# A hybrid trunk on one core: products 6 and 7 set apart by a quarter, the multiplications by embedding weights in ordered steps, the residual's copy behind the copies of the first product

## The chip, the cores and the metric

The kernel runs on one core of one Trainium2 chip. The metric is the time of one execution on the device, in microseconds (us); smaller is better. Before the change three runs took 1029.31, 1035.53 and 1035.87 us, with a median of 1035.53. The engines have short names in the profile: PE multiplies matrices, DVE is the vector engine, ACT the scalar engine, POOL the general one, which here mostly issues DMAs, and SP issues the loads of weights.

## The reference

Two layers over 256 tokens of 2048 features, in float32. An even layer (HGRN2 and RG-LRU side by side) and an odd one (mLSTM) are each followed by an output projection onto the residual and by a gated embedding of each layer's own. Cut to what matters:

```python
D_MODEL = 2048; SEQ = 256; DEPTH = 2; PLE_DIM = 256
h = x
for i in range(DEPTH):
    hn = rmsnorm(h, e_norm[j] if i % 2 == 0 else o_norm[j])
    if i % 2 == 0:
        u = hn @ e_w_in[j]
        ...
        y = jnp.concatenate([ya, yb], axis=-1).astype(h.dtype)
        mix = y @ e_w_out[j]
    else:
        u = hn @ o_w_in[j]
        ...
        yc = (head_rmsnorm(yc, c_norm[j]) * jax.nn.sigmoid(og.astype(jnp.float32))
              * jax.nn.silu(z.astype(jnp.float32)))
        mix = yc.astype(h.dtype) @ o_w_out[j]
    h = h + mix
    pl = rmsnorm(p[i].astype(h.dtype) @ ple_w[i], ple_norm[i])
    h = h + jax.nn.sigmoid(h @ ple_gate_w[i]) * pl
return rmsnorm(h, final_norm)
```

## The kernel before

**How weights become products.** A weight is float32 and is used as a sum of a high and a low half. SP loads a piece of 128 x 1024 into a tile `raw` (a ring of five), ACT casts it to the high half `whi` (L136, or L218 in the products below), and DVE subtracts to get the low half `wlo` (L137, L219). Both halves have rings of four. The activations `ahl` are split in the same way. PE then makes three matmuls of 128 x 512 for each product of two pieces: high by high, low by high, high by low (L208 to L210, or L232). A stop of PE therefore has a chain behind it: a cast on ACT, a subtraction on DVE.

**Plain blocks and seven products.** A projection works on blocks of 512 columns. Its first blocks are plain: four quarters of the 2048 features, one after the other. Pairs of blocks go through `seven` (L283), which replaces the eight products of a 2 x 2 split of one quarter (or of two) by seven, made of sums of weight pieces and of activations (`combos`, L246, whose results are the tiles `q`), and treats the remaining quarters plainly. It has four PSUM banks: A, F and B of the pool called `mm`, and E of the pool called `mx`. Every pair starts with the first product into A. ACT then copies A to F (L335) and -F to B (L336), where `home` is given also the residual tile to E (L338), and the second product goes into E. The rest follows a string, one letter at a time: a digit is that product (5, 6 and 7 into B, 2 into A, 4 into F), a or b is a plain quarter of the first block (into A and F) or the second (into E and B), A or F hands that result on, and a dot is a call of `pump`. Product 5's and product 6's sums in B are copied out by ACT (`keep`, L317), product 7's is subtracted by DVE (`soon`, L313).

**The four uses.** The string for one quarter, `ORDERS[1]`, is used by the even output projection (weights `in_eo`), the gate of the first embedding (`in_g0`), the first pair of the odd layer's output gates (`in_oog`) and the odd output projection (`in_oo`). Only the last gives `home`: there E starts from a quarter of the residual, `hq[3]`, which the odd layer has stored to DRAM and loads back on POOL's queue (`hq<-dh`).

**What sets the order.** Each engine runs its instructions in a fixed order, which a scheduler makes from the dependences and from priorities (`high_priority`). `issue_after(x)` keeps an instruction behind x on x's engine. Work of other kinds sits in generators, one per lane; each `pump` takes one step of every lane and keeps its instructions behind the last ones noted for each engine:

```python
def pump():
    with ExitStack() as behind:
        for ins in last.values():
            behind.enter_context(tc.issue_after(ins))
        for lane in list(lanes):
            step(lane)
```

One such lane is `pg`: the multiplications of the first layer's embedding by its norm's weights (`ple_gain`, L541). Another brings finished parts of the residual from token-major to feature-major form, by a hop through DRAM on POOL's queue (`across`, L669: one store at L672 and four loads into `r` at L675). The weights of the norm come by `row` (L532): two DMAs on POOL's queue, each of which spreads half a row over all partitions. `row` was called where the lane is started, so its DMAs were no step and had no place kept. The sums of the next layer's gates (`gate_sums`, L1134, matmuls at L1140) are a step of a lane too.

Of the kernel before, what the change touches and what calls it, by code (L numbers as in the profile page):

```python
# [15 lines left out]
AF = mybir.ActivationFunctionType  # L16
# [6 lines left out]
KT = D // P  # L23
EPS = 1e-6
RSQRT_MAGIC = 0x5F3759DF
ORDERS = {1: "a5a6.7b2.4aAFbb", 2: "a5.2aA64.7F.bb"}


_PRM = [
# [15 lines left out]
def trunk(ctx: ExitStack, tc: tile.TileContext, a, out):  # L45
    nc = tc.nc
    v, s, gp, te, sy = nc.vector, nc.scalar, nc.gpsimd, nc.tensor, nc.sync
# [17 lines left out]
    def start(lane, gen):  # L65
        lanes.setdefault(lane, []).append(gen)
# [9 lines left out]
# [6 lines that stand above are left out]
# [40 lines left out]
    def block(src, c, n):  # L122
        return src[c * P:(c + n) * P].rearrange("(p n) -> p n", p=P)
# [90 lines left out]
    def split_weights(r):  # L214

        hi, lo = (wp.tile([P, 1024], F32R, name=n, tag=n) for n in ("whi", "wlo"))
        with tc.high_priority(offset=400):
            last["act"] = s.copy(hi, r).ins  # L218
            last["dve"] = v.tensor_tensor(out=lo, in0=r, in1=hi.bitcast(F32), op=ALU.subtract).ins  # L219
        return hi, lo  # L220

    def product(o, stat, parts, first=False, end=False):

        n = 2 * len(parts)
        for k in range(n):
            xh, xl = (x[k] for x in stat)
            wh, wl = (x[:, (k % 2) * 512:(k % 2 + 1) * 512] for x in parts[k // 2])
            for i, (x, y) in enumerate(((xh, wh), (xh, wl), (xl, wh))):
                with ExitStack() as behind:
                    if k + i == 0:  # L230
                        behind.enter_context(tc.issue_after(last["pe"]))
                    last["pe"] = te.matmul(o, x, y, start=(first and k + i == 0), stop=(end and k == n - 1 and i == 2),  # L232
                                           skip_group_check=True).ins

    def stationary(act, js, hf):
        return [[tokens(act[j][x], k, hf) for j in js for k in range(2)] for x in range(2)]

    def plain(w, j, kq, act, ps, first=(False, False), end=False):

        parts = load_weights(w[4 * j + kq])  # L240
        for hf in range(2):
            product(ps[hf], stationary(act, (2 * kq, 2 * kq + 1), hf), parts, first[hf], end)
            if hf == 0:
                pump()
# [38 lines left out]
    def seven(w, j, act, qs, kqs, room, part, home=None, order=None):  # L283

        def src(b, side, kq):
            return block(w[4 * (j + b) + kq], side * 1024, 1024)

        def load(tile_of, b, side):
            tiles = []
            for kq in kqs:  # L290
                t = tile_of()
                sy.dma_start(out=t, in_=src(b, side, kq))
                tiles.append(t)
            return tiles

        def ring():
            return wp.tile([P, 1024], F32, name="raw", tag="raw", bufs=5)

        def split(tiles):
            return [split_weights(t) for t in tiles]  # L300

        def add(x, y):
            with tc.high_priority(offset=400):
                for xi, yi in zip(x, y):
                    v.tensor_tensor(out=xi, in0=xi, in1=yi, op=ALU.add)

        def add_loaded(x):
            for xi, kq in zip(x, kqs):
                gp.dma_start(out=xi, in_=src(1, 0, kq), accum_op=ALU.add)

        def soon(out, in0, in1, op):
            with tc.high_priority(offset=450):
                v.tensor_tensor(out=out, in0=in0, in1=in1, op=op)  # L313

        def keep(out, bank):
            with tc.high_priority(offset=450):
                s.copy(out, bank)  # L317

        def quadrant(side, hf):
            return stationary(act, [2 * kq + side for kq in kqs], hf)  # L320

        def combo(n):
            return [[t for kq in kqs for t in qs[n, kq][x]] for x in range(2)]

        acc = len(kqs) == 2
        rest = [kq for kq in range(4) if kq not in kqs]
        E = px.tile([P, 512], F32, name="mx", tag="mx")
        A, F, B = (pm.tile([P, 512], F32, name="mm", tag="mm") for _ in range(3))
        b5, g = part(), part()
        X = load(room, 0, 0)  # L330
        product(A, quadrant(0, 0), split(X), True)
        if acc:
            add_loaded(X)
        with tc.high_priority(offset=450):
            s.copy(F, A)  # L335
            s.activation(B, F, AF.Copy, scale=-1.0)  # L336
            if home is not None:
                s.copy(E, home)  # L338
        Y = load(room, 1, 1)
        product(E, combo(4), split(Y), home is None)  # L340
        W = X
        if not acc:
            W = load(ring, 1, 0)
            add(Y, W)
            add(W, X)
        rows = [list(rest), list(rest)]
        did = set()
        for op in order or ORDERS[len(kqs)]:
            if op in "ab":
                b = "ab".index(op)  # L350
                kq = rows[b].pop(0)
                plain(w, j + b, kq, act, ((A, F), (E, B))[b], end=not rows[b])
            elif op == "5":
                product(B, combo(1), split(W))
                add(X, Y)
                if acc:
                    add_loaded(Y)
                keep(b5, B)
            elif op == "6":
                product(B, combo(2), split(X))  # L360
                keep(g, B)
            elif op == "2":
                Z = load(ring, 0, 1)
                product(A, quadrant(1, 0), split(Z))
            elif op == "4":
                product(F, quadrant(1, 1), split(X))
            elif op == "7":
                product(B, combo(3), split(Y))
                soon(b5, B, b5, ALU.subtract)
            elif op == ".":  # L370
                pump()
            elif op == "A":
                yield 0, 0, A
            elif op == "F":
                soon(b5, F, b5, ALU.subtract)
                yield 0, 1, b5
            did.add(op)
            if op in "26" and {"2", "6"} <= did:
                add(X, Z)
        if home is None:  # L380
            soon(g, E, g, ALU.add)
            yield 1, 0, g
        else:
            soon(home, E, g, ALU.add)
            yield 1, 0, None
        yield 1, 1, B
# [145 lines left out]
    def row(pool, tag, bufs, i):  # L532

        halves = []
        for b in range(2):
            t = pool.tile([P, 1024], F32, name="row", tag=tag, bufs=bufs)
            gp.dma_start(out=t, in_=a["rows"][i, b * 1024:(b + 1) * 1024].partition_broadcast(P))
            halves.append(t)
        return halves

    def ple_gain(pls, rows):  # L541
        yield
        for g in range(4):
            for pl in pls[g]:
                v.tensor_tensor(out=pl, in0=pl, in1=rows[g // 2][:, (g % 2) * 512:(g % 2 + 1) * 512], op=ALU.mult)
                yield

    def to_features(h, c, act, gain, name, more=None):

# [64 lines left out]
    def small(n, name, rows=P):  # L614
        return cp.tile([rows, n], F32, name=name)
# [7 lines left out]
    pls = embed(a["pw"], None, lambda: p0.tile([P, 512], F32, name="pl", tag="pl"),  # L623
                lambda: sy.dma_start(out=prm, in_=a["prm"]))
# [82 lines left out]
    def gate_tok(w, j, act, u):  # L707
# [7 lines left out]
    mx, e0, e1, lb, omb, sp, ez, z2, pol, sp8, spm8 = (small(8, n) for n in (  # L715
        "mx", "e0", "e1", "lb", "omb", "sp", "ez", "z2", "pol", "sp8", "spm8"))
# [402 lines left out]
    pe0 = []  # L1119
    act = out_proj(hq, mixed(), "fe")  # L1120
    e0 = pe0[0]
    start("pg", ple_gain(pls, row(e0, "row", 2, 0)))

    gr = e0.tile([P, KT, 16], F32, name="gr")
    sy.dma_start(out=gr, in_=a["ogf"])
# [45 lines left out]
    with tc.tile_pool(name="m1", bufs=2) as m1:  # L1171
# [198 lines left out]
        def part():  # L1370
            n = len(turn) % 4
            turn.append(n)
            return store_of[n // 2][:, n % 2 * 512:(n % 2 + 1) * 512]
# [7 lines left out]
        def pair(w, jj, two):  # L1381
            return seven(w, jj, acth, qs, (0, 1) if two else (0,), chain2 if two else chain, part)
# [51 lines left out]
        pls = embed(a["pw1"], pact, pl_half)  # L1434
# [250 lines left out]
```

## Time and profile before

| | us |
|---|---|
| median of three runs | 1035.53 |
| lowest and highest run | 1029.31, 1035.87 |
| the profiled execution | 1035.23 |
| its span, first to last instruction | 1033.5 |
| busy: DVE, ACT, POOL | 824.0, 650.9, 105.2 |

The span is what the page covers; the 1.7 us between it and the execution's time lie around it. In a timeline a row is: start, duration, engine, line and operation, result <- operands, shapes, count, and in brackets how long the engine had been idle and what ended that. Matmuls overlap: one lasts 0.39 us, but a running PE starts the next before that has ended, so intervals are taken from start to start. Where a row of the kernel before names L545, L590 or L703, the kernel after has the same work two lines further down.

### The profile page before, as it was taken

What the parts mean: (1) busy time and instruction counts of PE and PEld (TensorE: products, weight loads), DVE (VectorE), ACT (ScalarE), POOL (GpSimd) and SP (SyncE); (2) the same over time, 40 slices, a digit from 0 to 9 for tenths busy, and PEclk for the clock granted to TensorE, in tenths of its full rate; (3) what the DMA queues carried; (4) which work ended last, traced back from release to release, by engine and by line L of the source; (5) the groups of instructions that cost most, each with busy time, mean ns of one, the idle gap of its engine ahead of it and who ended that gap; (6) DMA issues with size and microseconds to landing.
All of it is one profiled execution on the core that took longest, in us unless ns stands there. A gap on an engine that the chain in (4) does not pass through costs nothing.

```text
span 1033.5 us, 14486 instructions
## 1 busy us (share of the span) xinstructions
PE 1015.4 (98%) x5170; PEld 840.6 (81%) x5170; DVE 824.0 (80%) x1208; ACT 650.9 (63%) x933; POOL 105.2 (10%) x190
## 2 busy tenths in 40 slices
PE   9999999999999899999999999999999998999996
PEld 8888888888888778878888888888888886878886
DVE  7858968969685898888559987878889995986684
ACT  7675555586964455676557876666676866454562
POOL 0111101011111111022021100001001120102000
PEclk9999999999999999999999999999999999999999
DMA  9987756567688698588798756466879796679652
GB/s 363 328 232 243 224 165 204 184 194 243 225 258 310 210 314 267 167 290 277 242 287 243 232 175 202 126 231 186 284 184 289 220 283 259 197 256 283 229 184 82
DMA packets 69672, 242.14 MB, mean 234 GB/s; under 512 B 9024, under 2 KB 10432, under 8 KB 69600
## 3 DMA queue, kind: packets, MB, share of 16 engines
q1 hardware_dynamic: 54720, 193.36, 57.0%
q0 software_dynamic: 14448, 47.33, 16.6%
q8 instruction: 40, 0.66, 0.3%
q10 hardware_dynamic: 432, 0.52, 0.1%
q14 instruction: 32, 0.26, 0.1%
HBM read 221.26 MB, written 19.92 MB: 233 GB/s over the span
## 4 chain that ended last, share of the span: by engine, by line
PE 90%; DMA 4%; ACT 1%; DVE 1%; issue 1%; POOL 1%; ACTq 0%; DVEq 0%; POOLq 0%
PE mm L232 21%; PE mm L208 16%; PE mm L209 16%; PE mm L210 16%; PE mx L232 5%; PE mx L209 3%; PE mx L210 3%; PE mx L208 3%; DMA hq<-dh 2%; DMA ducn<-w 1%; DMA row<-in_rows_dram 1%; PE nu L1319 1%; PE mm L1510 1%; PE mm L1509 1%; PE mm L1511 1%
## 5 line engine op out<-in xcount | busy, mean ns | idle before, releaser
L136 ACT CAST whi<-raw 128x1024 fp32r<-128x1024 f32 (+1 forms) x317 | 331.1, 1048 | 229.3 <-PE mm L210 115.7
L137 DVE TENSOR_TENSOR wlo<-raw,whi 128x1024 fp32r<-128x1024 f32 (+1 forms) x317 | 381.4, 1213 | 115.2 <-ACT whi L136 106.7
L208 PE MATMUL mm<-whi,ahl 128*128 128x512 f32 x768 | 300.3, 391 | 0.0
L209 PE MATMUL mm<-wlo,ahl 128*128 128x512 f32 x768 | 299.3, 390 | 0.0
L210 PE MATMUL mm<-whi,ahl 128*128 128x512 f32 x768 | 298.9, 389 | 0.0
L232 PE MATMUL mm<-whi,ahl 128*128 128x512 f32 x552 | 177.1, 390 | 0.0
L208 PEld LDWEIGHTS mm<-whi,ahl 128*128 128x128 f32 x768 | 144.2, 188 | 30.3 <-issue 0.4
L210 PEld LDWEIGHTS mm<-whi,ahl 128*128 128x128 f32 x768 | 144.2, 188 | 30.2
L209 PEld LDWEIGHTS mm<-wlo,ahl 128*128 128x128 f32 x768 | 144.2, 188 | 29.8 <-DVE wlo L137 0.8
L232 PEld LDWEIGHTS mm<-whi,ahl 128*128 128x128 f32 x552 | 103.6, 188 | 22.1 <-issue 0.4
L232 PE MATMUL mm<-wlo,ahl 128*128 128x512 f32 x276 | 107.6, 390 | 1.4 <-DVE wlo L137 1.4
L219 DVE TENSOR_TENSOR wlo<-ch,whi 128x1024 fp32r<-128x1024 f32 x56 | 67.5, 1218 | 7.6 <-ACT whi L218 6.3
L218 ACT CAST whi<-ch 128x1024 fp32r<-128x1024 f32 x56 | 58.4, 1050 | 17.9 <-PE mm L232 10.7
L208 PE MATMUL mx<-whi,ahl 128*128 128x512 f32 x160 | 62.9, 393 | 2.9 <-ACT whi L136 2.9
L209 PE MATMUL mx<-wlo,ahl 128*128 128x512 f32 x160 | 63.3, 395 | 2.0 <-DVE wlo L137 2.0
L210 PE MATMUL mx<-whi,ahl 128*128 128x512 f32 x160 | 62.8, 393 | 0.0
L232 PEld LDWEIGHTS mm<-wlo,ahl 128*128 128x128 f32 x276 | 51.8, 188 | 12.6 <-DVE wlo L137 1.8
L232 PE MATMUL mx<-whi,ahl 128*128 128x512 f32 x144 | 47.3, 389 | 0.0
L232 PE MATMUL mm<-whi,q 128*128 128x512 f32 x120 | 41.0, 394 | 2.7 <-ACT pr L317 2.7
L208 PEld LDWEIGHTS mx<-whi,ahl 128*128 128x128 f32 x160 | 30.4, 190 | 9.8 <-ACT whi L136 3.4
L209 PEld LDWEIGHTS mx<-wlo,ahl 128*128 128x128 f32 x160 | 30.4, 190 | 9.1 <-DVE wlo L137 2.7
L210 PEld LDWEIGHTS mx<-whi,ahl 128*128 128x128 f32 x160 | 30.5, 190 | 6.3
(377 smaller groups left out, 1229.5 us busy)
## 6 DMA issues: line engine op xcount, KB each, us to landing
raw<-in_ew_dram SPq DMA_DIRECT2D x64, 512.0 KB, 5.1
raw<-in_g_dram SPq DMA_DIRECT2D x62, 512.0 KB, 4.8
raw<-in_oqk_dram SPq DMA_DIRECT2D x32, 512.0 KB, 5.4
raw<-in_ov_dram SPq DMA_DIRECT2D x32, 512.0 KB, 3.7
raw<-in_eo_dram SPq DMA_DIRECT2D x30, 512.0 KB, 5.3
raw<-in_oo_dram SPq DMA_DIRECT2D x30, 512.0 KB, 6.0
raw<-in_oog_dram SPq DMA_DIRECT2D x24, 512.0 KB, 4.3
raw<-in_oz_dram SPq DMA_DIRECT2D x20, 512.0 KB, 4.9
```

What stands on the lines that cost most here:

```text
L136: last["act"] = s.copy(h, r).ins
L137: last["dve"] = v.tensor_tensor(out=l, in0=r, in1=h.bitcast(F32), op=ALU.subtract).ins
L208: te.matmul(ps[hf], xh, wh, start=(k == 0), stop=False)
L209: te.matmul(ps[hf], xh, wl, start=False, stop=False)
L210: last["pe"] = te.matmul(ps[hf], xl, wh, start=False, stop=(k == KT - 1)).ins
L218: last["act"] = s.copy(hi, r).ins
L219: last["dve"] = v.tensor_tensor(out=lo, in0=r, in1=hi.bitcast(F32), op=ALU.subtract).ins
L232: last["pe"] = te.matmul(o, x, y, start=(first and k + i == 0), stop=(end and k == n - 1 and i == 2), skip_group_check=True).ins
L1319: te.matmul(ps[:, 0:n], x[:, i, o:o + P], y[:, b, i], start=(b == 0 and x is sh and y is vh), stop=(b == hf and y is vl))
L1509: te.matmul(o, xh, wh, start=(k == 0), stop=False)
L1510: te.matmul(o, xh, wl, start=False, stop=False)
L1511: last["pe"] = te.matmul(o, xl, wh, start=False, stop=(k == KT - 1)).ins
```

## The change

It has three parts.

The string for one quarter has a new order. Product 2, a quarter of the first block and A's result now stand between products 6 and 7; product 4 comes behind 7 and a quarter of the second block; and there is one dot more.

The residual's copy into E is now issued behind the second of ACT's two copies of the first product.

`ple_gain` gets a function in place of the tiles. The load of the row is now the lane's first step, with a step of its own, and the multiplications go two to a step.

```diff
-ORDERS = {1: "a5a6.7b2.4aAFbb", 2: "a5.2aA64.7F.bb"}
+ORDERS = {1: "a5a6.2aA7b.4F.bb", 2: "a5.2aA64.7F.bb"}
...
             s.copy(F, A)
-            s.activation(B, F, AF.Copy, scale=-1.0)
-            if home is not None:
-                s.copy(E, home)
+            with tc.issue_after(s.activation(B, F, AF.Copy, scale=-1.0).ins):
+                if home is not None:
+                    s.copy(E, home)
...
-    def ple_gain(pls, rows):
+    def ple_gain(pls, load):
+        rows = load()
+        yield
         yield
         for g in range(4):
             for pl in pls[g]:
                 v.tensor_tensor(out=pl, in0=pl, in1=rows[g // 2][:, (g % 2) * 512:(g % 2 + 1) * 512], op=ALU.mult)
-                yield
+            yield
...
-    start("pg", ple_gain(pls, row(e0, "row", 2, 0)))
+    start("pg", ple_gain(pls, lambda: row(e0, "row", 2, 0)))
```

**PE in the even output projection.** Before, the rows go from product 6 to product 7 and on to b; both products are into bank B, which is `mm_3423` here, and E is `mx_3420`. The operands `q4_3148` and `q4_3096` are sums of activations.

```order
L232 MATMUL mm_3423<-wlo_3539,q4_3148 128x512
L232 MATMUL mm_3423<-whi_3538,q4_3148 128x512
L232 MATMUL mm_3423<-whi_3549,q4_3096 128x512
L232 MATMUL mm_3423<-wlo_3550,q4_3096 128x512
L232 MATMUL mm_3423<-whi_3549,q4_3096 128x512 x2
L232 MATMUL mm_3423<-wlo_3550,q4_3096 128x512
L232 MATMUL mm_3423<-whi_3549,q4_3096 128x512
L232 MATMUL mx_3420<-whi_3561,ahl_2981 128x512
```

After the change the same place reads as follows; `mm_3421` is bank A.

```order
L232 MATMUL mm_3423<-wlo_3539,q4_3148 128x512
L232 MATMUL mm_3423<-whi_3538,q4_3148 128x512
L232 MATMUL mm_3421<-whi_3551,ahl_2791 128x512
L232 MATMUL mm_3421<-wlo_3552,ahl_2791 128x512
L232 MATMUL mm_3421<-whi_3551,ahl_2791 128x512 x2
L232 MATMUL mm_3421<-wlo_3552,ahl_2791 128x512
L232 MATMUL mm_3421<-whi_3551,ahl_2791 128x512
L232 MATMUL mm_3421<-whi_3563,ahl_3297 128x512
```

Product 2 follows product 6, then the 24 matmuls of a quarter a into A and F (the last row is its first), and only then product 7 into B. The other three uses have the same order.

**DVE, from the even output projection to the first gate.** Before, the first two multiplications by the row stood between two pairs of `wlo` of the even output projection:

```order
L1034 TENSOR_TENSOR xr<-r,tt 128x512 x2
L151 TENSOR_TENSOR ahl<-xr,ahl 128x2x256 x2
L137 TENSOR_TENSOR wlo<-raw,whi 128x1024 x2
L545 TENSOR_TENSOR pl<-pl,row 128x512 x2
L137 TENSOR_TENSOR wlo<-raw,whi 128x1024 x2
L590 TENSOR_TENSOR hq<-mm,hq 128x512
```

After, all eight stand in the first gate:

```order
L137 TENSOR_TENSOR wlo<-raw,whi 128x1024
L572 TENSOR_TENSOR ahl<-r,ahl 128x256 x4
L137 TENSOR_TENSOR wlo<-raw,whi 128x1024 x4
L547 TENSOR_TENSOR pl<-pl,row 128x512 x5
L137 TENSOR_TENSOR wlo<-raw,whi 128x1024
L547 TENSOR_TENSOR pl<-pl,row 128x512
L137 TENSOR_TENSOR wlo<-raw,whi 128x1024
L572 TENSOR_TENSOR ahl<-r,ahl 128x256 x4
L547 TENSOR_TENSOR pl<-pl,row 128x512 x2
```

The other six were in the first gate before as well, one or two at a time between pairs of `wlo`. The first four of the eight read the first half of the row, the other four the second. On POOL the two row DMAs stood ahead of the first hop of the even output projection, and stand behind its fourth and last hop now.

**ACT in the odd output projection.** Before, the residual's copy stood among casts of plain quarters:

```order
L436 ACTIVATE sq,pss<-pl 128x512 x3
L136 CAST whi<-raw 128x1024 x2
L338 COPY mx<-hq 128x512
L703 ACTIVATE xr<-r,prm 128x256 x3
L150 CAST ahl<-xr 128x2x256
L703 ACTIVATE xr<-r,prm 128x256
```

After, it stands with the two copies of the first product:

```order
L136 CAST whi<-raw 128x1024 x2
L335 COPY mm<-mm 128x512
L218 CAST whi<-raw 128x1024
L336 ACTIVATE mm<-mm 128x512
L338 COPY mx<-hq 128x512
L136 CAST whi<-raw 128x1024 x2
```

Nothing else of ACT stands between the `L335` and the `L338` than the cast and the copy shown.

## The prediction

> **What bounds the kernel now.** I read the page's busy times first, then the table of waits of TensorE (PE), then the timelines around those waits.
>
> ```profile
> span 1033.5 us, 14486 instructions
> PE 1015.4 (98%) x5170; PEld 840.6 (81%) x5170; DVE 824.0 (80%) x1208; ACT 650.9 (63%) x933; POOL 105.2 (10%) x190
> ```
>
> PE is busy for 98% of the span. Only a moment in which PE stands can give time back, and all such moments together are 1033.5 - 1015.4 = 18.1 us. The table of waits names those of PE; its columns are total us, times, longest us.
>
> ```profile
> PE mx L208 <- ACT whi L136: 2.9, 1, 2.9
> PE mm L232 <- ACT pr L317: 2.7, 4, 0.7
> PE mx L209 <- DVE wlo L137: 2.0, 2, 1.3
> PE mm L232 <- DVE wlo L137: 1.4, 1, 1.4
> ```
>
> Nothing else behind its start holds PE for long enough to be listed. The diff touches all four rows, and each part of it is costed at its place. Idle time alone undercounts a wait, because the matmuls behind it start more slowly, so I count from start to start.
>
> **The order string.** The first of its four uses is in the even output projection.
>
> ```profile
> 362.70 0.39 PE L232 MATMUL mm<-wlo,q 128*128 128x512 f32 x1
> 362.93 0.39 PE L232 MATMUL mm<-whi,q 128*128 128x512 f32 x1
> 363.99 0.51 PE L232 MATMUL mm<-whi,q 128*128 128x512 f32 x1 [0.68 <-ACT pr L317]
> 364.33 0.47 PE L232 MATMUL mm<-wlo,q 128*128 128x512 f32 x1
> ```
>
> A running PE starts a matmul every 0.23 us (362.70 to 362.93). Product 6 ends with the row of 362.93, and product 7 may overwrite bank B only when ACT has copied 6 out of it. From 362.93 to 364.33 stand two intervals: 1.40 us in place of 0.46, so 0.94 us are lost, and the table of waits says four times: 3.8 us. In the new string product 2 (6 matmuls) and a quarter a (24) stand between them, 30 x 0.23 = 6.9 us of work that doesn't touch B, against 1.06 us in which the copy was done. The copy is hidden behind them, and the whole 3.8 us goes. Behind 7 the next user of B is still the quarter b, at its old distance, so 7's subtraction on DVE is no later for it. Product 2's weights are asked for two loads earlier; a term for that is under the rivals.
>
> The string has one pump more, so ordered steps are issued earlier. One of them is work on PE itself: the sums of the next layer's gates (L1140) in the first gate, which read what a transpose hop through DRAM brings.
>
> ```profile
> 456.06 2.22 POOL L675 DMA_DIRECT2D r<-dfg  x4 [5.02 <-ACT xr L561]
> DMA to landing us min/median/max: 3.1/4.1/5.0
> 469.00 1.07 PE L1140 MATMUL st<-r,wg 128*32 128x256 f32 x16
> ```
>
> The hop is issued until 458.28 and has landed by 458.28 + 5.0 = 463.3 at the latest. PE reached the sums at 469.00. Now 12 matmuls fewer stand ahead of them, so it comes there 2.7 us earlier, at 466.3. There are 3.0 us to spare, and I take 0; had the hop been late by the whole 5.0 again, the price would be 2.0.
>
> **The row load, where it goes away.** In the even output projection DVE stood for a row of gains, and work for PE was queued behind it.
>
> ```profile
> 326.59 10.63 DMA row<-in_rows_dram
> 337.25 1.29 DVE L545 TENSOR_TENSOR pl<-pl,row 128x512 f32<-128x512 f32 x2 [7.48 <-DMA row<-in_rows_dram]
> 338.10 0.39 PE L208 MATMUL mx<-whi,ahl 128*128 128x512 f32 x1
> 339.74 0.50 PE L209 MATMUL mx<-wlo,ahl 128*128 128x512 f32 x1 [1.25 <-DVE wlo L137]
> 340.08 0.40 PE L210 MATMUL mx<-whi,ahl 128*128 128x512 f32 x1
> 347.84 0.39 PE L232 MATMUL mm<-whi,ahl 128*128 128x512 f32 x1
> 349.99 0.40 PE L232 MATMUL mm<-whi,ahl 128*128 128x512 f32 x1
> ```
>
> The row was 10.63 us under way, DVE waited 7.48 of them, and the low halves wlo behind it came too late twice. From 338.10 to 340.08 two intervals take 1.98 us in place of 0.46, and from 347.84 to 349.99 they take 2.15: 1.5 + 1.7 = 3.2 us. Both multiplications and the load leave this place, so DVE is at the casts some 8 us earlier; I take -3.2.
>
> **The row load, where it goes to.** It is issued behind the last hop of that projection, and five of the multiplications stand ahead of a pair of wlo in the first gate.
>
> ```profile
> 401.21 2.18 POOL L675 DMA_DIRECT2D r<-dfe  x4 [5.91 <-ACT whi L136]
> DMA to landing us min/median/max: 8.0/9.3/11.1
> 406.46 2.59 DVE L137 TENSOR_TENSOR wlo<-raw,whi 128x1024 fp32r<-128x1024 f32 x2 [0.86 <-ACT whi L136]
> 417.62 1.06 ACT L136 CAST whi<-raw 128x1024 fp32r<-128x1024 f32 x1 [0.30 <-PE mm L210]
> ```
>
> In the times of before, the hop's four issues end at 403.39. The two row DMAs follow at about 403.9 and 404.5, and the second needs up to 11.1 us: 415.6. DVE comes to the multiplications at 409.05 and is held there; the fifth, the only one of them on the second row, takes 0.6 us (1.29/2 above): 416.2. With both rows at the median of 9.3 it is 416.2 too, for then the first lands at 413.2 and five multiplications follow it. The first wlo behind them takes 2.59/2 = 1.3: 417.5. PE needs it at 417.62 + 0.23 = 417.85, since the cast of 417.62 begins when PE has left the pair before. The second wlo (behind one more multiplication) is there at 417.5 + 0.6 + 1.3 = 419.4, against 417.85 + 6 x 0.23 = 419.2. So a wait of 4 to 7 us on DVE just fits at the slowest landing on record, to 0.2 us, and I take 0; at 8.0 there is about 1 us to spare. The upper end is in the rivals.
>
> **The residual's copy, where it goes away.** In the odd output projection ACT stood at the copy of the residual into bank E, long before E was needed.
>
> ```profile
> 870.67 0.59 ACT L338 COPY mx<-hq 128x512 f32<-128x512 f32 x1 [8.37 <-DMA hq<-dh]
> 873.93 1.03 ACT L136 CAST whi<-raw 128x1024 fp32r<-128x1024 f32 x1
> 871.70 0.39 PE L210 MATMUL mm<-whi,ahl 128*128 128x512 f32 x1
> 875.01 0.50 PE L208 MATMUL mx<-whi,ahl 128*128 128x512 f32 x1 [2.93 <-ACT whi L136]
> 876.27 0.79 PE L209 MATMUL mx<-wlo,ahl 128*128 128x512 f32 x1 [0.76 <-DVE wlo L137]
> 876.87 0.63 PE L210 MATMUL mx<-whi,ahl 128*128 128x512 f32 x1
> 879.74 0.40 PE L208 MATMUL mx<-whi,ahl 128*128 128x512 f32 x1
> 876.20:879.60 3.40, 3.33 (x8) 2.65 (x9) 3.40 (x6) 2.73 (x5) 0.00 (x0) 0.50 0.63 173
> ```
>
> PE stood from 872.09 to 875.01 for a cast that was queued behind the copy, and then the granted clock fell: the last row is a window of 3.4 us, in which the clock column reads 0.50. From 871.70 to 879.74 there are ten intervals (seven of them in that window): 8.04 us in place of 2.30, so 5.7 us were lost. Now nothing with a DMA's wait stands there: ACT is free 8 us earlier, and the work queued behind the copy (four activations, two casts, 3.3 us from 870.67 to 873.93) is done before PE asks. I take the whole 5.7.
>
> **The residual's copy, where it goes to.** It is now the third of ACT's copies after product A, and the product into E has to wait for it.
>
> ```profile
> 895.20 0.40 PE L232 MATMUL mm<-whi,ahl 128*128 128x512 f32 x1
> 895.43 0.40 PE L232 MATMUL mx<-whi,q 128*128 128x512 f32 x1
> 895.63 0.57 ACT L335 COPY mm<-mm 128x512 f32<-128x512 f32 x1 [0.31 <-PE mm L232]
> 896.11 1.05 ACT L218 CAST whi<-raw 128x1024 fp32r<-128x1024 f32 x1
> 897.06 0.59 ACT L336 ACTIVATE mm<-mm 128x512 f32<-128x512 f32 x1
> 897.57 1.04 ACT L136 CAST whi<-raw 128x1024 fp32r<-128x1024 f32 x1
> ```
>
> A's last matmul starts at 895.20, and the first of E followed at once. Now the copy (0.59 us) takes ACT's place of 897.57 and ends at 898.16; 0.05 us later, as after L317 above, PE starts E at 898.21. That is 2.78 us late, and the next matmul starts 0.1 later than usual (0.34 us, as from 363.99 to 364.33): +2.9 us. Nothing covers this, because PE takes its products in order. Idle, PE stands there for 2.6 us, from 895.60.
>
> **Sum.** -3.8 - 3.2 - 5.7 + 2.9 = -9.8 us. The profiled execution took 1035.23, so 1025.4; the median of the three runs, 1035.53, lies 0.3 above it, which gives 1025.7 for a median. A measurement of this kernel tells about 1% from no change, 10.4 us, so the bound of "faster" is 1025.2: the forecast sits on it.
>
> **The rivals.**
>
> The clock falls after E's wait. Half the clock cost 3.4/2 = 1.7 us in the window shown above. For it: an idle stretch of 2.93 us, and 0.76 more, came before that window. Against it: the stretch here is 2.6 us alone, 1.1 shorter than those two together. Time: 1027.4. The Trainium skill ("TensorE: Matmul & The Clock Gate", Part 1) states that the clock halves after at least one idle window of about 3.4 us and that this window runs free of the kernel. By that rule no fall follows 2.6 us and the sum stays 1025.7; but the trace shows a fall after 2.93, so the rule is not strict here, and the rival keeps its chance.
>
> The rows land late in the first gate. Another transfer that POOL issued took 16.64 us:
>
> ```profile
> 854.00 16.64 DMA hq<-dh
> ```
>
> If the second row took that long, it would land at 404.5 + 16.6 = 421.1, the first wlo would be there 1.9 later, at 423.0, and PE would stand 5.2 us. Time: 1030.9. Against it is that six row DMAs landed in 8.0 to 11.1 us.
>
> The odd projection's gain doesn't come: what kept PE there is also late for another reason, and the 5.7 us stay while E's 2.9 us are added. Time: 1031.4. Against it is that the row of 870.67 names one wait of 8.37 us, longer than all of PE's loss there.
>
> The end on the other side: slower than before. In each of the four uses the load for product 2 takes a slot of the ring of five two loads earlier and keeps it until the sixth product's sum is made, so a later quarter's load starts late and its cast comes late. At 9.8/4 = 2.5 us in each use the gain is gone, and from (9.8 + 10.4)/4 = 5.0 the kernel is slower by over 1%. With a cast as late as in the odd projection, 5.7 in each use: 1025.7 + 22.8 = 1048.5. Against it:
>
> ```profile
> ACT whi L136 <- PE mm L210: 115.7, 109, 4.1
> ```
>
> The casts wait for PE to leave their slots, 109 times, and for raw weights nowhere long enough to head the table.
>
> **How the numbers follow.** The forecast has 0.70; the clock 0.09, the late rows 0.09, the odd projection 0.07, the ring 0.05. The forecast's own range is 1023 to 1028.5, some 2.7 to either side for the median's own movement, and a little under half of it lies below 1025.2: 0.33 faster. The rest of it and the three rivals that end within 1% give 0.37 + 0.25 = 0.62 for no change that can be told; the ring's 0.05 is slower. For 8 in 10 the forecast's 0.70 isn't enough, so the range takes in the clock, the late rows and the odd projection. Below, all gains without E's wait give 1035.5 - 12.7 = 1022.8, and 2.3 for the median's movement (the lowest of the three runs was 1029.31) make 1020.5; above, it ends at 1031.5.
>
> **What would show it.** Right: the waits of PE name L317 no more; no DVE wait for a row before 350 us; ACT's L338 stands behind L336 without a DMA's wait, and PE's longest listed wait is one of about 2.6 us for it, with the clock at 1.00 behind it; DVE waits 4 to 7 us for the row in the first gate, and PE doesn't. Wrong: PE waits for wlo near 414 us (times of after), a granted clock of 0.5 behind E, a wait for raw weights at product 2, or the cast L136 late again in the odd projection.

## The result, and the profile after

Over eleven runs each, the kernel after took 1029.57 us in the median (1025.77 to 1031.47) and the kernel before 1035.53 (1029.31 to 1036.9). The ratio is 0.9945, with a 95% interval of 0.9928 to 0.9963: some 6 us faster, where 9.8 were forecast. The time lies within the range, and within 1% of the time before; the interval lies below 1, so the gain is small but clear. Of all the runs in this document one, of the multiplications alone, took 2330.02 us, and the ratio there leaves it out.

The profiled execution of the kernel after took 1031.47 us and was the slowest of the eleven, so what it shows as lost lies at the upper end. The page's first lines and the table of waits of PE (total us, times, longest) answer to those shown of before:

```profile
span 1029.7 us, 14491 instructions
PE 1014.8 (99%) x5170; PEld 842.2 (82%) x5170; DVE 824.3 (80%) x1208; ACT 648.6 (63%) x933; POOL 105.1 (10%) x190
```

```profile
PE mx L232 <- ACT mx L338: 2.6, 1, 2.6
PE mx L208 <- ACT whi L136: 1.0, 1, 1.0
PE mx L506 <- ACT whi L475: 1.0, 1, 1.0
PE st L98 <- PEq L1678: 0.8, 1, 0.8
PE mx L209 <- DVE wlo L137: 0.8, 1, 0.8
```

The four rows of before are gone: nothing waits for L317, and the waits for `whi` and `wlo` that stand here under L208 and L209 are at another place than before. The first row is the price that was forecast for E. The timeline of PE shows it:

```profile
888.87 0.39 PE L232 MATMUL mm<-whi,ahl 128*128 128x512 f32 x1
891.86 0.50 PE L232 MATMUL mx<-whi,q 128*128 128x512 f32 x1 [2.61 <-ACT mx L338]
892.20 0.39 PE L232 MATMUL mx<-wlo,q 128*128 128x512 f32 x1
```

From 888.87 to 892.20 two intervals take 3.33 us in place of 0.46: 2.9 us, as worked out.

The rows under L208 and L209 are new. They belong to the end of the first gate. In the timeline of ACT before the change, two casts stand ahead of the activations (L561) that read the third hop of that gate:

```profile
488.06 1.05 ACT L136 CAST whi<-raw 128x1024 fp32r<-128x1024 f32 x1 [2.82 <-PE mm L210]
489.42 1.06 ACT L136 CAST whi<-raw 128x1024 fp32r<-128x1024 f32 x1 [0.30 <-PE mm L210]
490.38 1.30 ACT L561 ACTIVATE xr<-r,prm 128x256 f32<-128x256 f32 x3
```

After the change the activations (now L563) stand ahead of the casts; ACT, then PE:

```profile
481.42 1.04 ACT L136 CAST whi<-raw 128x1024 fp32r<-128x1024 f32 x1
488.44 1.31 ACT L563 ACTIVATE xr<-r,prm 128x256 f32<-128x256 f32 x3 [5.98 <-DMA r<-dfg]
491.23 3.88 ACT L136 CAST whi<-raw 128x1024 fp32r<-128x1024 f32 x4
```

```profile
490.91 0.39 PE L210 MATMUL mx<-whi,ahl 128*128 128x512 f32 x1
492.32 0.50 PE L208 MATMUL mx<-whi,ahl 128*128 128x512 f32 x1 [1.02 <-ACT whi L136]
493.58 0.50 PE L209 MATMUL mx<-wlo,ahl 128*128 128x512 f32 x1 [0.76 <-DVE wlo L137]
497.80 0.40 PE L208 MATMUL mx<-whi,ahl 128*128 128x512 f32 x1
```

ACT stands 5.98 us for the hop, and the casts queued behind it begin at 491.23, when PE has none left. Between 490.91 and 497.80 there are 13 intervals: 6.89 us in place of 3.0. So 3.9 us were lost here. Some 1.6 of them are the clock, which fell to 0.5 for one window behind the two stops (its row is shown below): from 494.15 to 497.80 nine intervals take 3.65 us in place of 2.04.

One more difference is in the profiled execution and not in the change: the same matmul, the first behind an early attention step, starts 2.0 us later.

```profile
96.28 0.50 PE L208 MATMUL mm<-whi,ahl 128*128 128x512 f32 x1
```

```profile
98.25 0.50 PE L208 MATMUL mm<-whi,ahl 128*128 128x512 f32 x1
```

The first row is of before, the second of after. Ahead of it the two kernels run the same work, and the delay comes from the first matmuls: they wait 1.0 us for a cast (L506 in the table above), and the trace's record of the full clock begins at 9.66 us in place of 5.79. With it the two profiles balance: -9.8 as forecast, +3.9 and +2.0 make -3.9, and 1031.47 - 1035.23 is -3.8. Compared matmul by matmul, PE gained 4.0 us behind `L317` (0.9 to 1.2 in each use), 3.3 at the row and 5.8 at the copy's old place, and lost 2.9 at its new one, 4.0 at the hop and 2.0 at the start; behind PE's last matmul the rest of the program took 0.6 us longer.

### The profile page after: what moved, and what is told of

It is laid out like the page before. It is cut to its first block, busy times and chain, and to the rows that moved or that the text cites. A ratio compares the mean times of both kernels' runs of the same rounds, so it can differ in the third digit from the quotient of the medians.

```text
span 1029.7 us, 14491 instructions
## 1 busy us (share of the span) xinstructions
PE 1014.8 (99%) x5170; PEld 842.2 (82%) x5170; DVE 824.3 (80%) x1208; ACT 648.6 (63%) x933; POOL 105.1 (10%) x190
## 4 chain that ended last, share of the span: by engine, by line
PE 94%; DMA 2%; issue 2%; ACT 1%; POOL 0%; DVE 0%; ACTq 0%; POOLq 0%
PE mm L232 21%; PE mm L208 17%; PE mm L209 17%; PE mm L210 17%; PE mx L232 5%; PE mx L209 3%; PE mx L210 3%; PE mx L208 3%; PE mm L506 1%; PE mx L506 1%; PE nu L1321 1%; DMA r<-dfg 1%; PE mm L1512 1%; PE mm L1511 1%; PE mm L1513 1%
## 5 line engine op out<-in xcount | busy, mean ns | idle before, releaser
L137 DVE TENSOR_TENSOR wlo<-raw,whi 128x1024 fp32r<-128x1024 f32 (+1 forms) x317 | 381.5, 1214 | 125.8 <-ACT whi L136 118.1
L208 PE MATMUL mm<-whi,ahl 128*128 128x512 f32 x768 | 300.3, 391 | 0.0
L209 PE MATMUL mm<-wlo,ahl 128*128 128x512 f32 x768 | 299.0, 389 | 0.0
L208 PEld LDWEIGHTS mm<-whi,ahl 128*128 128x128 f32 x768 | 144.2, 188 | 30.3 <-issue 0.4
L209 PEld LDWEIGHTS mm<-wlo,ahl 128*128 128x128 f32 x768 | 144.2, 188 | 29.1
L208 PE MATMUL mx<-whi,ahl 128*128 128x512 f32 x160 | 62.9, 393 | 1.0 <-ACT whi L136 1.0
L209 PE MATMUL mx<-wlo,ahl 128*128 128x512 f32 x160 | 63.1, 394 | 0.8 <-DVE wlo L137 0.8
L208 PEld LDWEIGHTS mx<-whi,ahl 128*128 128x128 f32 x160 | 30.4, 190 | 7.9 <-ACT whi L136 1.4
L209 PEld LDWEIGHTS mx<-wlo,ahl 128*128 128x128 f32 x160 | 30.3, 189 | 7.4 <-DVE wlo L137 1.1
```

What stands on the lines that cost most here:

```text
L137: last["dve"] = v.tensor_tensor(out=l, in0=r, in1=h.bitcast(F32), op=ALU.subtract).ins
L208: te.matmul(ps[hf], xh, wh, start=(k == 0), stop=False)
L209: te.matmul(ps[hf], xh, wl, start=False, stop=False)
```

## Experiments

Each kernel was timed against the kernel before, run beside it on the same chip; ratios are to that. They were run in three sets, and the kernel before had medians of 1034.51 to 1035.53 us in them and in the result. Kernels of different sets are therefore compared by their ratios; the intervals of the ratios often overlap, so a difference of 2 or 3 us between two of them is an estimate with a wide margin.

**One dot less.**

```diff
-ORDERS = {1: "a5a6.2aA7b.4F.bb", 2: "a5.2aA64.7F.bb"}
+ORDERS = {1: "a5a6.2aA7b.4Fbb", 2: "a5.2aA64.7F.bb"}
```

> The changed kernel with one dot less in the string, the one behind F (4F.bb becomes 4Fbb). Theory: that dot lets the third hop of the first gate be read one pump earlier, so ACT's activations L563 stand ahead of two casts, ACT waits 6.0 us for the hop and PE loses 3.9 us at 490.9 us; without the dot the two casts come first again, PE loses nothing there, and the median falls from 1029.6 to about 1025.7 us. Rival: the hop itself comes later in the changed kernel (8.3 us on its way) and holds PE wherever its activations stand; then PE still loses 3 us or more near 490 us and the median stays at 1029 to 1030.

Measured: 1029.27 us, ratio 0.9943 (0.9924 to 0.9962). The theory held at its place and fell in its time; the rival's time came, but not by the rival's way. In this kernel's profile ACT has two casts ahead of the third hop's activations again and PE loses nothing near 490 us, but ACT waits for the hop before that one, and PE with it:

```profile
462.30 0.51 ACT L563 ACTIVATE xr<-r,prm 128x256 f32<-128x256 f32 x1 [4.59 <-DMA r<-dfg]
```

```profile
463.79 0.50 PE L232 MATMUL mx<-whi,ahl 128*128 128x512 f32 x1 [1.39 <-ACT whi L136]
465.05 0.50 PE L232 MATMUL mx<-wlo,ahl 128*128 128x512 f32 x1 [0.76 <-DVE wlo L137]
```

The clock fell behind these two stops as well, to 0.50 for the window from 465.95, and PE lost 4.2 us in all. In the changed kernel's profile ACT waited 2.9 us at that same place and PE just got through. So there are two places in the first gate, the second hop and the third, where the new string puts L563 ahead of casts that PE needs soon; whether PE is hit depends on when the hop lands, and that differs from execution to execution.

**The string alone.** The kernel before, with the new string and nothing else.

> The kernel before with the new string alone. Theory: the four waits of 0.94 us behind L317 go (-3.8), and the wait for the third hop comes (+3.9): 1035.5, within 1 us of the kernel before, with a wait of L563 for r<-dfg of some 6 us on ACT. Rival: the wait for the hop comes from the moved multiplications, not from the string; then ACT does not wait there and the time is 1031.7 us.

Measured: 1033.57 us, ratio 0.9981 (0.9964 to 0.9999). That is 2.0 us by the ratio and 1.5 by the medians, of 3.8, between the theory and its rival. In its profile ACT does wait for both hops, without the other two parts:

```profile
ACT xr L561 <- DMA r<-dfg: 8.2, 2, 4.6
```

In the three profiles with the old string ACT waits once for a hop, for 0.6 to 1.8 us, and PE doesn't. The longer wait belongs to the string. Here the two waits cost PE 1.7 us, so the price is less than the whole 3.9.

**The residual's copy alone.**

```diff
-            s.activation(B, F, AF.Copy, scale=-1.0)
-            if home is not None:
-                s.copy(E, home)
+            with tc.issue_after(s.activation(B, F, AF.Copy, scale=-1.0).ins):
+                if home is not None:
+                    s.copy(E, home)
```

> The kernel before with the residual's copy moved alone. Theory: the 5.7 us at 871.7 go and 2.9 come at E: 1032.7 us, L338 without a DMA's wait, PE waits 2.6 us for it. Rival: the stop at 871.7 has a second cause and stays, with 2.9 more at E: 1038.4 us.

Measured: 1033.1 us, ratio 0.9986 (0.9973 to 0.9999): 2.0 us by the medians and 1.4 by the ratio, in place of 2.8. In its profile the stop near 870 us is gone and the wait at E is 2.6 us, but behind it the clock fell, as the first rival of the prediction had it. A table by windows shows it; the columns are the window, its length, busy us of PE, PEld, DVE, ACT and POOL with counts, then the granted clock.

```profile
887.89:891.30 3.41, 0.80 (x4) 0.52 (x4) 3.41 (x4) 2.52 (x4) 2.21 (x4) 1.00 0.41 86
891.30:894.70 3.40, 3.40 (x10) 2.63 (x9) 2.78 (x5) 1.04 (x1) 0.00 (x0) 0.50 1.00 269
```

PE was busy for 0.80 us of the first window, which holds the whole wait; in the second it runs ten matmuls, where it runs 15 or 16 at full clock. This cost 1.6 us on top of the stop's 2.9.

**The multiplications alone.** The kernel before, with `ple_gain` and its call as in the change.

> The kernel before with the multiplications in ordered steps alone. Theory: the two waits of PE for wlo at 338 and 348 us go: 1032.3 us, no wait of DVE for the row before 350 us. Rival: the multiplications, now five in a row in the first gate, cost PE there what they gave at 338: 1035.5 us.

Measured: 1032.54 us, ratio 0.9967 (0.9952 to 0.9982). That is 3.4 us by the ratio and 2.5 by the medians; 3.2 were worked out. In its table of waits no wait of PE for `wlo` is longer than 0.5 us, and the stop of the odd projection, which this kernel keeps, heads it:

```profile
PE mx L208 <- ACT whi L136: 3.6, 1, 3.6
```

**The hops read later.** The changed kernel, with another count of pumps between a hop's issue and its reading.

```diff
-        yield from across(w, r, f"d{name}{c}", 6)
+        yield from across(w, r, f"d{name}{c}", (6, 10, 7, 7)[c] if name == "fg" else 6)
```

> The changed kernel, with the hops of the first gate read more pumps after their issue (10 in place of 6 for the second, 7 for the third and fourth). Theory, formed after e1_no_dot: not one dot but the new string as a whole puts ACT's L563 for the second and for the third hop ahead of casts that PE needs, and whether a hop lands in time differs from run to run; with the reads behind those casts ACT does not hold them up, PE loses nothing at 462 or 490 us, and the median falls from 1029.5 to about 1025.7 us. Rival: the missing 4 us are not the hops but the granted clock and the start, which differ from run to run; then the median stays at 1029 to 1030.

Measured: 1026.6 us, ratio 0.9919 (0.9898 to 0.9941), 2.7 us below the changed kernel's ratio; the two intervals overlap a little. In the profile PE has no wait near 462 or 490 us. ACT still stands 3.7 us for the fourth hop, at 493.73, but PE doesn't. Of PE's waits, E's is the only one behind the start:

```profile
PE mx L232 <- ACT mx L338: 2.6, 1, 2.6
PE st L98 <- PEq L1678: 0.8, 1, 0.8
PE mx L506 <- ACT whi L475: 0.6, 1, 0.6
```

**The residual's copy earlier.** The changed kernel, with the copy behind the cast of the first product's weights and ahead of that product.

```diff
-        product(A, quadrant(0, 0), split(X), True)
+        parts = split(X)
+        if home is not None:
+            with tc.high_priority(offset=450), tc.issue_after(last["act"]):
+                s.copy(E, home)
+        product(A, quadrant(0, 0), parts, True)
...
-            with tc.issue_after(s.activation(B, F, AF.Copy, scale=-1.0).ins):
-                if home is not None:
-                    s.copy(E, home)
+            s.activation(B, F, AF.Copy, scale=-1.0)
```

> The changed kernel, with the residual's copy into E issued behind the cast of the first product's weights, where ACT has been idle and the residual has landed. Theory: E follows A at once, PE's wait of 2.6 us for L338 goes with the 0.3 behind it, and so does the fall of the clock that came behind that wait in e3_copy_only (1.7 us where it happens): 2.9 to 4 us faster than the changed kernel, about 1026 us. Rival: the copy there delays the next cast by its 0.5 us and PE waits for that instead; then less than 1 us is gained.

Measured: 1025.09 us, ratio 0.9904 (0.9879 to 0.9929), 4.2 us below the changed kernel's ratio (0.0041 x 1035). In the timeline E follows A at once:

```profile
882.65 0.40 PE L232 MATMUL mm<-whi,ahl 128*128 128x512 f32 x1
882.88 0.40 PE L232 MATMUL mx<-whi,q 128*128 128x512 f32 x1
```

The profiled execution was the fastest of its four runs, 1022.64 us. ACT waited for two hops in it and PE for neither; the other runs took up to 1027.04. No other profile of this kernel was kept, so that the hops spread these times is inferred; the next run bears it out.

**Both.** The two edits together.

> Both edits, of e5_lag and e6_copy_early, together. Theory: the gains add up, since the places are 400 us apart: 1029.5 - 3.8 - 2.9 to 4 = about 1022.5 us, 1.2% below the kernel before. Rival: as for the two alone; 1026 us or more.

Measured: 1022.66 us, ratio 0.9884 (0.9861 to 0.9907). The gains add up, to 6.3 us by the ratios where the two alone had 2.7 and 4.2, and the four runs lie between 1022.58 and 1023.29, where the eleven of the changed kernel lie 5.7 us apart. PE's one wait in the table is the one at its start:

```profile
PE st L98 <- PEq L1680: 0.8, 1, 0.8
```

This version beats the kernel before and, by the ratios, the changed kernel too: the two intervals don't meet.

**The copy in second place.** The kernel with the later reads, and the residual's copy directly behind the copy from A to F.

```diff
-            s.copy(F, A)
-            with tc.issue_after(s.activation(B, F, AF.Copy, scale=-1.0).ins):
+            with tc.issue_after(s.copy(F, A).ins):
                 if home is not None:
                     s.copy(E, home)
+            s.activation(B, F, AF.Copy, scale=-1.0)
```

> The kernel of e5_lag with the residual's copy one place further up on ACT, behind the first copy of the first product (bank A to F) and ahead of the cast and of the second copy. PE's wait for E then has two of ACT's operations in it in place of four: 0.5 + 0.6, so PE stands 1.1 us in place of 2.6. Theory: the clock fell behind windows of 3.41 us in which PE was busy for 0.80 and 1.63 us and not behind one of 1.80, so a window must be idle for half of its length; 1.1 us can't do that, the clock never falls there, and the kernel gains the 1.5 us of idle time and, on average over runs, another 1: about 1024.2 us, with its runs closer together than those of e5_lag (1025.35 to 1027.52). Rival: the clock has no part in the missing time; then only the 1.5 us come, 1025.1 us, with the same spread.

Measured: 1024.5 us (1024.14 to 1025.46), ratio 0.99 (0.9883 to 0.9916). PE stood 1.2 us for E (the copy is L337 in this kernel) and the clock stayed at 1.00:

```profile
885.67 0.50 PE L232 MATMUL mx<-whi,q 128*128 128x512 f32 x1 [1.17 <-ACT mx L337]
```

The median is 2.1 us below that of the later reads (2.0 by the ratios) and the runs are closer together (1.3 us apart, against 2.2), which leans to the theory. The two intervals overlap and there are four runs of each, so how much of the missing time the clock's falls make up stays open.

## Why the prediction was right, and where it was off

**The string's waits: right.** The four waits for L317 are gone in the changed kernel, and PE gained 4.0 us at their places, where 3.8 were worked out.

**The row load, where it goes away: right.** Alone, the part brought 3.4 us by the ratio and 2.5 by the medians, where 3.2 were worked out, and in its own profile and the changed kernel's PE gained 3.3 us there.

**The row load, where it goes to: the price was right, the wait was not there.** A wait of DVE of 4 to 7 us was expected, and in the changed kernel's profile there is none. The rows were issued behind the hop as expected, but landed in 6.7 and 9.2 us, and DVE's subtractions (`L137`) ahead of the multiplications ended at 406.43, some 1.5 us later than 409.05 less the 4.1 us gained until there; this execution had lost 2.0 us at its start. In five other profiles with the rows moved DVE does wait for them, 0.7 to 2.5 us, and PE in none. The timeline of DVE has no idle time ahead of the multiplications, and the second line is the rows' least, median and longest time to landing:

```profile
406.35 3.14 DVE L547 TENSOR_TENSOR pl<-pl,row 128x512 f32<-128x512 f32 x5
```

```profile
DMA to landing us min/median/max: 6.7/8.0/9.2
```

**The residual's copy, where it goes away: right.** No profile with the copy moved has a stop in that stage.

**The residual's copy, where it goes to: the stop was right, the clock was mis-sized.** The stop measured 2.9 us, as worked out. The clock stayed at 1.00 behind it in this profile, as forecast, but in that of the copy alone it fell. The fall was given a chance of 0.09, because 2.6 us of idle time seemed too few. The windows of the changed kernel say what matters:

```profile
490.94:494.35 3.41, 1.63 (x6) 0.86 (x5) 3.09 (x7) 3.41 (x5) 2.15 (x4) 1.00 0.62 179
494.35:497.77 3.42, 3.42 (x9) 2.63 (x8) 3.29 (x9) 0.76 (x1) 0.00 (x0) 0.50 0.86 232
...
886.84:890.25 3.41, 2.42 (x11) 1.68 (x9) 3.41 (x5) 2.80 (x4) 0.48 (x2) 1.00 0.39 156
890.25:893.66 3.41, 1.80 (x8) 1.49 (x9) 3.41 (x4) 1.67 (x4) 1.83 (x4) 1.00 0.75 217
893.66:897.10 3.44, 3.44 (x17) 2.83 (x16) 3.13 (x8) 0.94 (x1) 0.23 (x1) 1.00 1.03 258
```

A window in which PE was busy for 1.63 us, at the end of the first gate, was followed by one at 0.50. E's wait happened to be cut by the border of two windows, and the worse of them, with 1.80 us busy, was not. In the kernel with the copy alone the whole wait lay in one window, 0.80 us busy, and the clock fell. So the same 2.6 us cost 2.9 in one execution and 1.6 more in another. If the clock falls behind a window with less than some 1.7 us of busy time, as these three suggest, a wait of 2.6 us escapes only where the border leaves at most 1.7 us of it on either side: over 0.8 of 3.4 us, a quarter of the positions. That is an estimate. Against it, four profiles have a wait of 2.6 us at E, and three of them show no fall behind it: besides the changed kernel those with one dot less (2.17 and 2.05 us busy) and with the hops read later (1.95 and 2.26). So 0.09 was too low, but whether the chance is nearer a quarter or three quarters stays open.

**The pump: the step that failed.** "There are 3.0 us to spare, and I take 0" was worked out for the step's work on PE, the gate sums, and these were indeed not held; 12 matmuls fewer stood ahead of them, as worked out. The same lane has work on ACT, the activations L563 that read the hop, and these stand in a strict row with the casts that feed PE. A step that is issued earlier relative to those casts makes ACT stand for the hop, and PE behind it. The order of ACT in the first gate showed it before any run: L563 ahead of two casts where L561 stood behind them. I followed the moved step on one only of the engines that it uses. Nor was the extra pump the whole of it: with one dot less, as many as before, the second hop's read still stood ahead of casts. What it costs is not one number, but the loss follows ACT's wait. At the second hop waits of 0.9 and 2.9 us cost PE nothing, 3.7 cost 0.5 and 4.6 cost 4.2; at the third, 3.7 cost nothing, 4.6 cost 1.2 and 6.0 cost 4.0 (the copy early, the string alone, one dot less and the changed kernel, matmul by matmul). By the ratios, putting the reads behind the casts is worth 2.7 us of the changed kernel (0.9945 to 0.9919), and 2.1 with the copy early (0.9904 to 0.9884).

**The sum.** 1025.7 us were forecast. Adding 2.7 us for the hops gives 1028.4, and the measured median is 1029.57. The clock's falls behind E could make up some of the remaining 1.2, but they were not timed by themselves: with the reads late, the early copy brings 3.6 us by the ratios (0.9919 to 0.9884), 0.7 more than the stop's 2.9. The rest stays open. The forecast's own range, 1023 to 1028.5, was missed. The wide one held, but in part by luck: its upper part was there for three rivals, and what filled it was a loss that none of them named.

**The rivals.** The rows landed in time for PE, the odd projection's gain came, and no product waited for its raw weights. Of the rivals only the clock's was seen, in the profile of the copy alone. Of the signs that were to show the prediction right, only DVE's wait for the rows was missing from the changed kernel's profile, and none of the signs of being wrong stood in it: no sign looked at ACT in the first gate. The Trainium skill ("TensorE: Matmul & The Clock Gate", Part 1) asks for an idle window of about 3.4 us before the clock halves. The trace agrees on the window's length (3.41 us), but not on how much of it must be idle: 2.6 us were enough, and so were two stops of 1.02 and 0.76 us.

## What to carry to other kernels

When a step of background work moves, look on every engine that it uses for what now stands behind it there, above all on the engine that feeds the bound one: a read of a transfer, one cast too early, holds up all the casts behind it. Where a copy must stand ahead of a product, put it where its engine is idle and its data has landed, not merely away from the place where it waits; here that was worth some 4 us. A kernel whose runs scatter can have a race between a transfer and a need: with the copy early, moving the reads brought four runs from 4.4 us apart to 0.7.

## What the runs showed of the hardware

The clock fell without one long stop. At the end of the first gate PE stood for 1.02 and 0.76 us, with one matmul between, and ran the next 3.4 us at half clock, 1.6 us lost for 1.8 idle. In the ten profiles each window in which PE was busy for 1.63 us or less was followed by one at half clock, and no window that began at full clock with 1.80 us or more was. Once, in the multiplications alone, half clock lasted for two windows, 6.83 us. The windows lie on a grid of 3.41 us: the trace of the changed kernel has its next fall, behind PE's last matmuls, at 1023.42 us, which is 155 windows behind the 494.35 shown above. The grid has no fixed relation to the program. A border came 1.4 us behind the last matmul ahead of E's wait in the changed kernel and 0.2 us behind it in the copy alone, and the same wait cost 2.9 us in the one and 4.5 in the other.
